# Output stage of a hybrid decoder step: weight loads issued by ScalarE's queue instead of SyncE's

## The chip, the cores and the metric

One core of a Trainium2 chip. The metric is the device time of the whole program in microseconds, here the median of several runs; the profile is of one execution. The engines are named as the profile names them: PE (TensorE), PEld (its weight loads), DVE (VectorE), ACT (ScalarE), POOL (GpSimd) and SP (SyncE), which computes nothing and issues DMAs. Each engine works through its own instructions in order; an instruction that starts a DMA is one of them, and waits like any other until what it depends on is done.

## What is computed

One inference step of a decoder layer, for a prompt of 1024 tokens (with 16 meta tokens ahead of it) and for eight sampled sequences of 4 tokens. Two branches, stick-breaking attention and gated linear attention, share one input projection and one output projection:

```
h = rms_norm(x, norm_pre_g)
(q, k, v), sg, (gq, gk, gv, gf), gg = branch_inputs(h, w_in, w_alpha, b_alpha)
o_sb = sb_prompt(q, k, v, sb_bias)            # sb_sample for the sampled rows
o_gla, s_end = gla_prompt(gq, gk, gv, gf)
mixed = concat([o_sb * silu(sg), rms_norm(o_gla) * silu(gg)])
x = x + rms_norm(mixed @ w_out, norm_post_g)  # 1024 x 2048 @ 2048 x 2048, fp32
```

The outputs are y for both, and the new keys, values and states. The change is in the stage that computes `mixed @ w_out` and the last norm.

## The kernel before

The program projects, runs both branches, and ends with the output stage (from L1282, some 360 us of 2080). The gated rows of the prompt lie in DRAM as `md`, in blocks of 128 x 512 that hold `mixed` transposed.

**Seven products in place of eight.** The output is cut in 2 x 2 blocks, and the block product is done by seven products p, in the order 1, 2, 6, 5, 3, 7, 4, each for two column halves q of 512. Their right sides are blocks of `w_out` (p = 1, 2, 3) or differences of such blocks that an earlier stage left in DRAM as `td` (p = 5, 6, 7, 4); their left sides are "forms" (`form`, L1357): blocks of `md`, or sums of them, loaded by SP in `quarter` (L1291, tiles q).

**fp32 in three passes.** Each fp32 operand is split in a high part, a CAST on ACT, and a low part, the rest, a subtraction on DVE: L1339 and L1342 for a form, L1400 and L1401 for a weight tile. `product` (L1594 to 1596) multiplies high by high, high by low, and low by high.

**A step (p, q)** is `step` (L1600): eight values of k, and for each the function `weights` and twelve products of 128 x 512 in four PSUM banks (t = 0 to 3). `weights` takes one of four `wr` buffers (`oy` pool, 128 x 512 fp32, 256 KB), loads the weight tile into it (L1395), casts it (L1400) and subtracts (L1401) into one of four slots of `ring`. In steps with p = 1, 2, 7 and 3, every second k is followed by eight small products for the sampled rows (L1614, tile `sc`) that read the two raw `wr` tiles; these buffers are free only behind them. In the other steps a `wr` buffer is free after its subtraction. Such a step of two k is a "sampled pair" below.

**Evacuation.** After eight k, `take` reads the four banks: for p = 1 copies on ACT (L1444), for p = 2 DVE and ACT (L1448), for p = 4 an addition on DVE (L1465) and `done` (L1435 on ACT, L1436 on DVE). The next product with the same banks waits for that.

**What runs beside it.** `finish0` (L1508 to 1538) normalizes the first half of the rows during p = 7 and p = 4: it loads x (L1519, L1522), does L1529 on DVE and stores (L1530). `load_keep` runs `weights` eight times more, for p = 4 and q = 1, into tiles of their own ("kept" loads), so that the last step finds its weights ready; the tail (from `take_last`) works row block by row block. `gain` (L1425) loads the norm's factors. All these DMAs are issued by SP; only one store at the very end (L1588) is ACT's.

**What sets the order.** A scheduler orders the instructions of each engine at build time by data dependence and priority; `weights` runs under `urgent()`, a higher priority. `behind_ring` sets kept loads and x loads behind the newest ring load where both are on one engine's list. Four first loads of the stage (`firsts`, L1318) were issued earlier.

Of the kernel before, what the change touches and what calls it, by code (L numbers as in the profile page):

```python
# [84 lines left out]
def hybrid_step(ctx: ExitStack, tc: tile.TileContext, x_prompt, x_sample, cache_k, cache_v, state_gla,  # L85
# [3 lines left out]
    nc = tc.nc  # L89
# [3 lines left out]
    def urgent():  # L93
        return tc.high_priority(offset=URGENT)
# [97 lines left out]
    with tc.tile_pool(name="xp", bufs=2) as xp, tc.tile_pool(name="xps", bufs=5, space=PSUM) as xps:  # L192
# [109 lines left out]
        for c, (lo, hi) in enumerate(XCHUNKS):  # L302
            n = hi - lo
            for k in range(NK):
                ps = xps.tile([P, 512], F32, tag="tx", name=f"tx{c}_{k}")
                ks = slice(k % 8 * P, (k % 8 + 1) * P)
                for j, i in enumerate(TILES[c]):
                    xt = xts[i]
                    if len(xt) == 2:
                        src, ii = xt[k // 8][:, ks], ident[:]  # L310
                    else:
                        rs = slice(64 * (k // 8), 64 * (k // 8) + 48)
                        src, ii = xt[0][rs, ks], ident[rs, rs]
                    nc.tensor.transpose(ps[:, j * P:min((j + 1) * P, n)], src, ii)
                ins = act.activation(hh[k][:, lo:hi], ps[:, :n], AF.Copy, scale=gpre[:, k:k + 1]).ins
# [967 lines left out]
    with ExitStack() as out:  # L1283
# [90 lines left out]
        def behind_ring(ins):  # L1374
            tc.add_manual_dep(ins, newest[0].name, NOSYNC, reason="behind")
# [3 lines left out]
        def weights(p, q, k, dst=None):  # L1379
            with urgent():  # L1380
                to_ring = dst is None
                if to_ring:
                    j = next(turn) % 4
                    dst = [t[:, j * 512:(j + 1) * 512] for t in ring]
                wh, wl = dst
                if firsts:
                    r = firsts.pop(0)
                else:
                    r = oy.tile([P, 512], F32, tag="wr", name=f"wr{p}{q}_{k}")[:]
                    if p <= 3:  # L1390
                        r0, c0 = (1024 if p > 1 else 0) + P * k, (1024 if p == 3 else 0) + 512 * q
                        src = w_out[0, r0:r0 + P, c0:c0 + 512]
                    else:
                        src = td[{5: 0, 6: 1, 7: 2, 4: 3}[p]][:, k, q * 512:(q + 1) * 512]
                    ins = nc.sync.dma_start(r, src).ins  # L1395
                    if to_ring:
                        newest[:] = [ins]
                    else:
                        behind_ring(ins)
                act.copy(wh, r)  # L1400
                vec.tensor_tensor(wl, r, wh.bitcast(F32), ALU.subtract)  # L1401
            return wh, wl, r
# [197 lines left out]
        def step(p, q, banks, first, last):  # L1600

            c = {1: 0, 2: 0, 7: 1, 3: 1}.get(p)
            if p in (1, 3):
                SB[c, q] = ops.tile([P, 512], F32, tag="S", bufs=2, name=f"sc{c}{q}")
            raws = []
            for k in range(8):
                w = weights(p, q, k)
                for t in range(4):
                    product(banks[t], t, p, k, w[:2], first, last)
                if c is not None:  # L1610
                    raws.append(w[2])
                    if k % 2:
                        for j in range(4):
                            mm(SB[c, q][32 * j:32 * j + 32, :256], small[SAMPLE[p]][:, k - 1 + j // 2, :],  # L1614
                               raws[j // 2][:, j % 2 * 256:j % 2 * 256 + 256], start=p in (1, 3) and k == 1,
                               stop=p in (2, 7) and k == 7, skip_group_check=True)
                        raws = []
                W.beat()
            for t in range(4):
                take(p, q, t, banks[t])  # L1620
            if p in (2, 7):
                sample_y(SB[c, q], 2 * c + q)
# [3 lines left out]
        def load_keep():  # L1626

            keep.extend(slot(REGION["B"][i], f"keep{i}") for i in range(4))
            for k in range(8):
                kept.append(weights(4, 1, k, [keep[k // 2][:, (2 * (k % 2) + i) * 512:(2 * (k % 2) + i + 1) * 512] for i in range(2)])[:2])  # L1630
                yield 3
# [55 lines left out]
```

## Time and profile before

| | us |
|---|---|
| median of 3 runs | 2083.68 (2082.94 to 2086.64) |
| profiled execution, device time | 2083.24 |
| its span in the trace | 2081.5 |
| granted PE clock, mean | 0.998 |
| output stage, steps in full use of PE | 1722 to 1963 |
| steps p = 7 and p = 4 (q = 0), p = 7 (q = 1) | 1963 to 2046 |
| last step and tail | 2046 to 2081.5 |

Times of rows are microseconds from the start of the span. A timeline row reads: start, duration, engine, line, operation, output and input tiles, shapes, how many instructions the row stands for, and in brackets how long the engine was idle before it and what ended that. SPq and ACTq are the queues' own rows: the time that the engine spends to issue a DMA, not the transfer. A row of waits reads: engine and line that waited, for which engine, tile and line, microseconds in all, times, the longest.

### The profile page before, as it was taken

The numbers are of one execution on the slowest core, as the hardware profiler recorded it, in microseconds if no ns is written. First come the engines' busy times: TensorE is split into PE (matmuls) and PEld (weight loads), VectorE is DVE, ScalarE is ACT, GpSimd is POOL, SyncE is SP. The second block draws the span as 40 slices with busy tenths as digits, with TensorE's granted clock in tenths as the row PEclk, the third lists the DMA queues.
The fourth block names the chain that finished last, engine by engine and source line by source line (L and its number), as shares of the span: only waits on it lengthen the run. The fifth ranks groups of instructions, "written<-read, shape, count | busy, mean of one in ns | idle before, by whom it ended". The sixth has DMA issues, their size and how long they took to land.

```text
span 2081.5 us, 42052 instructions
## 1 busy us (share of the span) xinstructions
PE 2047.1 (98%) x12547; PEld 1861.3 (89%) x12547; DVE 1553.6 (75%) x6284; ACT 958.5 (46%) x2286; POOL 83.9 (4%) x303
## 2 busy tenths in 40 slices
PE   6999999999999999999999999999999999999997
PEld 5999999999999989999999999998888898787775
DVE  7368989889888989899898888978444346553566
ACT  7355555565655656433535345253433335442332
POOL 0012000101000010000000000000000000000000
PEclk9999999999999999999999999999999999999999
DMA  6355454555554442533333434335777765442376
GB/s 200 105 135 151 134 159 135 159 136 151 146 159 144 143 115 79 143 96 85 108 98 84 121 76 119 82 92 162 236 226 239 222 214 188 138 151 83 127 247 212
DMA packets 372878, 301.86 MB, mean 145 GB/s; under 512 B 44440, under 2 KB 313160, under 8 KB 372648
## 3 DMA queue, kind: packets, MB, share of 16 engines
q1 hardware_dynamic: 372344, 298.64, 49.2%
q8 instruction: 99, 1.62, 0.3%
q14 instruction: 131, 1.07, 0.2%
q10 hardware_dynamic: 304, 0.53, 0.1%
HBM read 241.75 MB, written 57.31 MB: 144 GB/s over the span
## 4 chain that ended last, share of the span: by engine, by line
PE 89%; DVE 6%; DMA 3%; ACT 2%; issue 1%; POOL 0%; SPq 0%; DVEq 0%; ACTq 0%; POOLq 0%
PE acc_g L344 6%; PE acc_g L345 6%; PE acc_g L346 6%; PE b L1594 4%; PE b L1595 4%; PE b L1596 4%; PE acc_k L344 3%; PE acc_k L345 3%; PE acc_k L346 3%; PE acc_q L344 3%; PE acc_q L345 3%; PE acc_q L346 3%; PE acc_v L344 3%; PE acc_v L346 2%; PE acc_v L345 2%; PE acc_gv L344 2%
## 5 line engine op out<-in xcount | busy, mean ns | idle before, releaser
L463 DVE SCALAR_TENSOR_TENSOR jk<-kp,qb 128x128 f32<-128x128 f32 x2048 | 591.9, 289 | 41.8 <-DMA qb<-qsd 1.1
L344 PE MATMUL acc_g<-hT,wh_g 128*128 128x368 f32 (+2 forms) x768 | 251.2, 327 | 0.0
L345 PE MATMUL acc_g<-hT,wh_g 128*128 128x368 f32 (+2 forms) x768 | 247.3, 322 | 0.0
L346 PE MATMUL acc_g<-hT,wl_g 128*128 128x368 f32 (+2 forms) x768 | 247.0, 322 | 0.0
L1594 PE MATMUL b<-ring,f 128*128 128x512 f32 x416 | 166.2, 401 | 3.5 <-DVE u L1465 1.8
L463 DVE DVE_READ_ACCUMULATOR jk<-kp,qb 128x1 f32 x2048 | 166.5, 81 | 0.0
L1595 PE MATMUL b<-ring,f 128*128 128x512 f32 x416 | 163.3, 392 | 0.7 <-DVE ring L1401 0.6
L1401 DVE TENSOR_TENSOR ring<-wr,ring 128x512 fp32r<-128x512 f32 x104 | 70.7, 689 | 124.7 <-ACT ring L1400 124.4
L1596 PE MATMUL b<-ring,f 128*128 128x512 f32 x416 | 162.9, 392 | 0.0
L344 PEld LDWEIGHTS acc_g<-hT,wh_g 128*128 128x128 f32 x768 | 144.3, 188 | 12.7 <-issue 11.0
L345 PEld LDWEIGHTS acc_g<-hT,wh_g 128*128 128x128 f32 x768 | 144.4, 188 | 1.1 <-issue 0.4
L346 PEld LDWEIGHTS acc_g<-hT,wl_g 128*128 128x128 f32 x768 | 144.3, 188 | 0.0
L1400 ACT CAST ring<-wr 128x512 fp32r<-128x512 f32 x104 | 64.0, 621 | 159.5 <-DMA wr<-in_w_out_dram 74.2
L344 PE MATMUL acc_gv<-hT,wh_gv 128*128 128x384 f32 (+1 forms) x384 | 129.9, 338 | 0.0
L344 PE MATMUL acc_k<-hT,wh_k 128*128 128x378 f32 (+1 forms) x384 | 127.6, 332 | 0.0
L344 PE MATMUL acc_q<-hT,wh_q 128*128 128x368 f32 (+2 forms) x384 | 125.4, 326 | 0.0
L345 PE MATMUL acc_k<-hT,wh_k 128*128 128x378 f32 (+1 forms) x384 | 125.4, 326 | 0.0
L346 PE MATMUL acc_k<-hT,wl_k 128*128 128x378 f32 (+1 forms) x384 | 125.2, 326 | 0.0
L346 PE MATMUL acc_gv<-hT,wl_gv 128*128 128x384 f32 (+1 forms) x384 | 124.5, 324 | 0.0
L345 PE MATMUL acc_gv<-hT,wh_gv 128*128 128x384 f32 (+1 forms) x384 | 124.5, 324 | 0.0
L345 PE MATMUL acc_q<-hT,wh_q 128*128 128x368 f32 (+2 forms) x384 | 123.6, 322 | 0.0
L346 PE MATMUL acc_q<-hT,wl_q 128*128 128x368 f32 (+2 forms) x384 | 123.5, 322 | 0.0
(447 smaller groups left out, 5295.8 us busy)
## 6 DMA issues: line engine op xcount, KB each, us to landing
kp<-in_cache_k_dram SPq DMA_DIRECT2D x512, 64.0 KB
vr<-in_cache_v_dram SPq DMA_DIRECT2D x64, 512.0 KB
tf<-in_w_out_dram SPq DMA_DIRECT2D x64, 256.0 KB
td<-tf SPq DMA_DIRECT2D x64, 256.0 KB
qb<-qsd SPq DMA_DIRECT2D x64, 256.0 KB
wr_g<-in_w_in_dram SPq DMA_DIRECT2D x64, 256.0 KB
wr<-td SPq DMA_DIRECT2D x64, 256.0 KB
wr<-in_w_out_dram SPq DMA_DIRECT2D x48, 256.0 KB
```

Source lines behind the costliest of these rows:

```text
L344: mm(acc[c][:, :n], wh, hh[k][:, lo:hi], start=(k == 0), stop=False)
L345: mm(acc[c][:, :n], wh, hl[k][:, lo:hi], start=False, stop=False)
L346: W.mark = mm(acc[c][:, :n], wl, hh[k][:, lo:hi], start=False, stop=(k == NK - 1)).ins
L463: ins = vec.scalar_tensor_tensor(jk[:], kp[:], 1.0, qbs[h, b][:, t, :], ALU.mult, ALU.mult, accum_out=zt[:, t, NPG - 1 - i:NPG - i])
L1400: act.copy(wh, r)
L1401: vec.tensor_tensor(wl, r, wh.bitcast(F32), ALU.subtract)
L1594: mm(bk[:], ah, wh, start=first and k == 0, stop=False, skip_group_check=True)
L1595: mm(bk[:], ah, wl, start=False, stop=False, skip_group_check=True)
L1596: mm(bk[:], al, wh, start=False, stop=last and k == 7, skip_group_check=True)
```

## The change

One line in `weights`: the load of a weight tile is issued by ACT instead of SP.

```
@@ -1392,7 +1392,7 @@
                         src = w_out[0, r0:r0 + P, c0:c0 + 512]
                     else:
                         src = td[{5: 0, 6: 1, 7: 2, 4: 3}[p]][:, k, q * 512:(q + 1) * 512]
-                    ins = nc.sync.dma_start(r, src).ins
+                    ins = nc.scalar.dma_start(r, src).ins
                     if to_ring:
                         newest[:] = [ins]
                     else:
```

108 loads of 256 KB move, 100 for the ring and 8 kept ones; the four of `firsts` stay on SP. The loads of forms, of x and of factors, and the stores, stay on SP too. SP's list goes from 3460 rows to 3352 and ACT's from 2157 to 2265.

On ACT, at the end of step p = 1 and the start of p = 2 (both q = 0). `f_3` is the last form tile of p = 2, `wr_7` the last weight tile of p = 1, `wr_0` and `wr_1` the first of p = 2; + is the kernel after.

```order
+L1339 CAST f_2_29395<-q_5_29422 128x512
 L1400 CAST ring_29253<-wr_7_29447 128x512
-L1339 CAST f_2_29395<-q_5_29422 128x512
 L1339 CAST f_3_29442<-q_6_29443 128x512
 L1339 CAST f_3_29442<-q_7_29467 128x512
+L1395 DMA wr_0_29481<-in_w_out_dram 128x512
+L1395 DMA wr_1_29497<-in_w_out_dram 128x512
 L1400 CAST ring_29253<-wr_0_29481 128x512
 L1400 CAST ring_29253<-wr_1_29497 128x512
```

The two loads now stand behind three casts of form 2; the four copies of L1444 follow the two casts of `wr_0` and `wr_1`, as before.

On SP, near the end of step p = 7, q = 1. `wr_7` with `td_128` is the last kept tile, `wr_6` and `wr_7` with `td_127` are the last ring tiles; `xr` and `xrs` are rows of x, and the stores to `out_dram` are finished rows.

```order
 L1519 DMA xr_2_31548<-in_x_prompt_dram 128x512
 L1530 DMA out_dram<-y_1_2_30997 128x512
-L1395 DMA wr_7_31541<-td_128 128x512
-L1395 DMA wr_6_31550<-td_127 128x512
+L1530 DMA out_dram<-y_0_3_30659 128x512
 L1522 DMA xrs_31422<-in_x_prompt_dram 128x512
 L1519 DMA xr_3_31569<-in_x_prompt_dram 128x512
-L1530 DMA out_dram<-y_0_3_30659 128x512
-L1395 DMA wr_7_31571<-td_127 128x512
 L1522 DMA xrs_31421<-in_x_prompt_dram 128x512
```

The loads are no longer behind a store on SP, and the next store moves up two places.

On ACT at the same place.

```order
 L1400 CAST ring_29253<-wr_4_31500 128x512
 L1400 CAST ring_29253<-wr_5_31521 128x512
+L1395 DMA wr_7_31541<-td_128 128x512
+L1395 DMA wr_6_31550<-td_127 128x512
 L1400 CAST keep_31048<-wr_7_31541 128x512
 L1400 CAST ring_29253<-wr_6_31550 128x512
+L1395 DMA wr_7_31571<-td_127 128x512
 L1400 CAST ring_29253<-wr_7_31571 128x512
 L1435 ACTIVATE jk_3_31595,yssq<-y_1_0_30796 128x512
```

The last kept load and the last two ring loads are issued between the casts, the very last one behind the cast of the tile before it.

More of the change, by code (lines that the diff above doesn't have):

```diff
@@ L1394, in weights @@
                         src = td[{5: 0, 6: 1, 7: 2, 4: 3}[p]][:, k, q * 512:(q + 1) * 512]
-                    ins = nc.sync.dma_start(r, src).ins
+                    ins = nc.scalar.dma_start(r, src).ins
                     if to_ring:
```

## The prediction

> **What bounds the kernel now.** I read the busy table of the page first, then the output stage cut into pieces by a table of windows, and then the waits of the queue that issues the loads. TensorE (PE) is busy nearly all the time.
>
> ```profile
> PE 2047.1 (98%) x12547; PEld 1861.3 (89%) x12547; DVE 1553.6 (75%) x6284; ACT 958.5 (46%) x2286; POOL 83.9 (4%) x303
> ```
>
> The change touches only the output stage, from about 1722 us on. Each row of the windows gives a stretch, then its length, then for PE, its weight loads, DVE, ACT and POOL the busy time, then the granted PE clock, the DMA share and GB/s.
>
> ```profile
> 1722.00:1963.00 241.00, 241.00 (x1187) 187.73 (x1185) 125.48 (x205) 93.64 (x177) 0.20 (x1) 1.00 0.42 134
> 1963.00:2046.00 83.00, 78.77 (x373) 57.86 (x366) 49.09 (x82) 28.13 (x60) 0.00 (x0) 0.98 0.73 237
> 2046.00:2072.10 26.10, 25.79 (x118) 20.15 (x117) 22.65 (x59) 7.13 (x24) 0.00 (x0) 1.00 0.54 184
> 2040.00:2045.00 5.00, 3.87 (x11) 2.86 (x12) 2.37 (x4) 1.35 (x3) 0.00 (x0) 0.75 0.71 218
> 2045.00:2050.00 5.00, 5.00 (x26) 3.54 (x25) 3.64 (x7) 2.10 (x6) 0.00 (x0) 0.91 0.98 311
> ```
>
> The reader is to see three things. In the first 241 us PE has no idle time (241.00 of 241.00), so an earlier load can win nothing there and a later one can only lose. The p=7 and p=4 steps, 1963 to 2046, hold 83.00 - 78.77 = 4.2 us of idle PE, and at the end of them a stretch of lowered clock (0.75, then 0.91), where PE counts as busy but is slow. After 2046 nothing that the change moves is left.
>
> SP issues all loads before. Rows: who waited, for what, us in all, times, longest.
>
> ```profile
> SPq L1395 <- PE sc L1614: 93.1, 27, 10.1
> SPq L1395 <- DVE ring L1401: 69.7, 42, 5.1
> SPq L1530 <- DVE y L1529: 8.1, 3, 4.0
> ```
>
> SP's waits at L1395 are mostly waits for a free buffer, which is no fault of SP: whichever queue issues the load has to wait for the same matmuls. Only the third row is time in which a store holds up loads that might have gone.
>
> **The change, part by part.** The issue itself: SP spends 319 to 333 ns on most of its loads, and ACT's own DMA at the end took 0.38 us.
>
> ```profile
> L1395 SPq DMA_DIRECT2D wr<-td x64: 319/320/1316, 1826.3 to 2040.9; - x64
> L1395 SPq DMA_DIRECT2D wr<-in_w_out_dram x44: 327/333/1937, 1738.7 to 1957.5; - x44
> 2077.35 0.38 ACTq L1588 DMA_DIRECT2D out_dram<-y  x1
> ```
>
> 108 loads (64 + 44; four more stay on SP) at 0.32 to 0.38 us are 35 to 41 us that go from SP to ACT. ACT is busy for 93.64 of 241 us and 28.13 of 83 us, so it has 202 us free beside PE's work and the time itself fits. What is not free is the order: ACT now stands at a load until its buffer is free, and casts and bank copies behind it wait, while a load stands behind casts that wait for other data. The slowest issues (1316 and 1937 ns) could come on either queue; I count them alike.
>
> *Term 1, end of step p=1 q=0 and start of p=2.* The order of the changed kernel puts loads 0 and 1 of p=2 on ACT behind the last two CASTs of form 2, and the four copies that empty the banks stay behind the casts of these loads. Before (SP, ACT, and the sampled products of PE):
>
> ```profile
> 1745.39 0.85 SPq L1395 DMA_DIRECT2D wr<-in_w_out_dram  x2
> 1751.22 0.80 SPq L1395 DMA_DIRECT2D wr<-in_w_out_dram  x2
> 1757.70 0.81 SPq L1395 DMA_DIRECT2D wr<-in_w_out_dram  x2
> 1751.35 1.98 ACT L1339 CAST f<-q 128x512 fp32r<-128x512 f32 x3
> 1755.59 0.62 ACT L1400 CAST ring<-wr 128x512 fp32r<-128x512 f32 x1 [2.26 <-DMA wr<-in_w_out_dram]
> 1756.89 2.04 ACT L1444 COPY u<-b 128x512 f32<-128x512 f32 x4
> 1757.04 0.64 PE L1614 MATMUL sc<-wr,small 128*32 128x256 f32 x8
> 1757.61 0.50 PE L1594 MATMUL b<-ring,f 128*128 128x512 f32 x1
> ```
>
> SP issued at 1751.22; ACT would be free of its three CASTs at 1751.35 + 1.98 = 1753.33, so the load starts 2.1 us later. The first cast came 1755.59 - 1751.22 = 4.37 us after its issue, so it comes at 1757.7, and the first copy 1.3 us behind it (1756.89 - 1755.59) at 1759.0 instead of 1756.89. PE's product at 1757.61 overwrites that bank, and the copy had ended only 0.2 us ahead of it. So this place loses 2.1 - 0.2 = 1.9 us. If the form's casts come 1.3 us sooner, as their data may once SP's queue holds no loads, 0.6 is left; if the next pair of loads, which then stands behind the 2.04 us of copies instead of 1757.70, uses up its reserve as well, it is some 3.5. **I take +1.9, bounds 0.6 to 3.5.**
>
> *Term 2, the other sampled pairs* (every two k of p=1, 2, 3 and 7; 21 of them outside terms 1 and 3). One from step p=1 q=1, before:
>
> ```profile
> 1813.86 1.91 SPq L1395 DMA_DIRECT2D wr<-in_w_out_dram  x2
> 1813.30 1.14 ACT L1339 CAST f<-q 128x512 fp32r<-128x512 f32 x2 [1.11 <-PE b L1596]
> 1817.18 0.62 ACT L1400 CAST ring<-wr 128x512 fp32r<-128x512 f32 x1 [2.74 <-DMA wr<-in_w_out_dram]
> 1817.83 0.69 DVE L1401 TENSOR_TENSOR ring<-wr,ring 128x512 fp32r<-128x512 f32 x1 [2.09 <-ACT ring L1400]
> 1820.34 0.39 PE L1595 MATMUL b<-ring,f 128*128 128x512 f32 x1
> ```
>
> The low half is ready at 1817.83 + 0.69 = 1818.52 and PE needs it at 1820.34, a reserve of 1.8 us. A load that must pass the two CASTs at 1813.30 would go at 1814.44, 0.6 later than SP's. If it had to pass both in full it would be 1.14 + 0.38 = 1.5 us, still inside 1.8. The cover is this reserve; beyond it each 0.1 us in 21 pairs is 2.1 us. The steps without samples have more room, since their buffers come free earlier. **I take +0.2, bounds 0 to 6.3** (0.3 us over in every pair).
>
> *Term 3, steps p=7 and p=4.* Here SP sends stores of finished rows and loads of x between the weight loads, in order. At the last place:
>
> ```profile
> 2032.63 0.64 PE L1614 MATMUL sc<-wr,small 128*32 128x256 f32 x8
> 2034.25 0.34 SPq L1530 DMA_DIRECT2D out_dram<-y  x1
> 2034.70 0.86 SPq L1395 DMA_DIRECT2D wr<-td  x2
> 2039.50 0.62 ACT L1400 CAST keep<-wr 128x512 fp32r<-128x512 f32 x1 [6.68 <-DMA wr<-td]
> 2040.23 0.62 ACT L1400 CAST ring<-wr 128x512 fp32r<-128x512 f32 x1
> 2040.15 0.69 DVE L1401 TENSOR_TENSOR keep<-wr,keep 128x512 fp32r<-128x512 f32 x1 [4.02 <-ACT keep L1400]
> 2040.90 0.49 PE L1594 MATMUL b<-ring,f 128*128 128x512 f32 x1 [1.39 <-ACT ring L1400]
> 2041.62 0.50 PE L1595 MATMUL b<-ring,f 128*128 128x512 f32 x1 [0.23 <-DVE ring L1401]
> 2042.43 0.58 PE L1595 MATMUL b<-ring,f 128*128 128x512 f32 x1
> 2045.80 0.43 PE L1594 MATMUL b<-ring,f 128*128 128x512 f32 x1
> ```
>
> The buffers were free when the sampled products ended, at 2032.63 + 0.64 = 2033.27; the loads went at 2034.70 because the store ahead of them waited for DVE. On ACT nothing is ahead of them (its CASTs had ended), so they go 1.4 us earlier, and the cast that PE waits for comes at 2038.8. The stall was 1.39 us, and the step to the low half took 0.72 us instead of the 0.34 of other places, 0.4 more; of these 1.8 about 0.2 is left. The eight products from 2042.43 to 2045.80 took 3.37 us where 8 x 0.227 = 1.8 is usual, so the lowered clock cost 1.55, which goes with the stall. That is -3.1. Then the next load is late: it takes the buffer that DVE gives back after the keep subtraction (2040.15 + 0.69, now 1.4 earlier, 2039.4), needs 3.1 us to land and 0.62 for its cast, and PE asks for it 2.72 us after 2039.5: 2043.1 against 2042.2, +0.9. So this place gives -2.2.
>
> [...]
>
> The other stalls of the stage, by their rows:
>
> ```profile
> 2016.59 0.62 ACT L1400 CAST keep<-wr 128x512 fp32r<-128x512 f32 x1 [5.41 <-DMA wr<-td]
> 2021.18 0.50 PE L1594 MATMUL b<-ring,f 128*128 128x512 f32 x1 [1.17 <-DVE u L1465]
> 2022.76 0.50 PE L1594 MATMUL b<-ring,f 128*128 128x512 f32 x1 [0.62 <-DVE u L1465]
> 1985.48 0.50 PE L1594 MATMUL b<-ring,f 128*128 128x512 f32 x1 [0.36 <-ACT ring L1400]
> ```
>
> The two of 1.17 and 0.62 follow from the kept load at 2016.59, behind which the cast of another ring load stood; that cast now goes ahead of it, but the bank's DVE additions (L1465) still stand behind the stores' arithmetic, so I take a third of their 1.8 off, -0.6. The one at 1985.48 goes, and a load of the same step that must pass a cast in its place costs as much: 0. In p=4 q=0 two L1435 passes now stand ahead of load 2: +0.3. **Term 3: -2.2 - 0.6 + 0.3 = -2.5, bounds -5.8 (all 4.2 of idle time and 1.55 of low clock) to +1** (the new order's stalls without the gain at the end).
>
> Sum: +1.9 + 0.2 - 2.5 = **-0.4 us**. On the profiled execution, 2083.24 us with its span of 2081.5, that is 2082.8; its own time lies 0.44 below the median of the three runs (2083.68), and on that median it is 2083.3, which I forecast.
>
> **The rivals.** (1) *All of the last stage's stalls go.* For it: the stage is the one place with idle PE, and DMA there is dense (0.73 of the engines), so loads that go their own way may also land sooner than behind SP's stores. Against: the buffers' releases and DVE's order are unchanged. Time: -5.8 + 0.6 = -5.2, 2078.5. [...]
>
> (2) *Slower, the ring runs behind.* Place: the 21 sampled pairs. Mechanism: ACT reaches a load late because a cast in front of it waits for its q tile or for a slot, and the load after it, its cast and the next load all follow on the same engine. It decides from a delay of 1.8 us per pair on. At 0.3 over it, 21 x 0.3 = 6.3, with +1.9 and a smaller gain of -1 in the end: +7.2, 2090.9. For it: the order does put a CAST ahead of the load in most of these steps. Against: 1.5 us is what two such casts cost.
>
> (3) *Slower, the first place at its bound and no gain at the end:* 3.5 + 1 = +4.5, 2088.2. It decides if the first cast of p=2 comes after 1759 and a stall of over 1 us stays before 2046.
>
> (4) *The loads are not sooner, whoever issues them:* SP's waits (93.1 and 69.7 us) are for buffers, and what is left is term 1: +1.9, 2085.6. [...]
>
> **How the numbers follow.** Chances: forecast 0.40, rival 1 0.19, rival 2 0.15, rival 3 0.16, rival 4 0.10. Within 0.2% (4.2 us, about what a measurement of this kernel tells from no change) lie the forecast and rival 4: 0.50; faster 0.19, slower 0.31. The range from 2078.3 to 2089.5 takes in rivals 1, 3 and 4 and the milder half of rival 2; left out are its rest and larger gains, under 2 in 10. The forecast's own range is 2080 to 2087.
>
> **What would show it.** In the profile of the changed kernel: the first L1444 copy starts about 2 us later against the sampled products before it, and PE idles 1 to 3 us there (term 1). In the rest of the stretch up to the p=5 and p=3 steps PE stays without idle time; idle time of a few tenths at each sampled pair means rival 2. In the p=7 and p=4 stretch the two loads near its end go right after the sampled products, the granted clock stays at 1.00, and a stall near 0.9 us comes one k later (term 3); if the clock still falls, the gain is nearly lost. A change of over 1 us after p=4's last ring product, or ACT issues much longer than 0.4 us, would make the whole working wrong.

## The result, and the profile after

| | before | after |
|---|---|---|
| median, us (lowest to highest, runs) | 2084.72 (2082.94 to 2089.36, 6) | 2095.14 (2090.84 to 2095.7, 6) |
| profiled execution, device time, us | 2083.24 | 2094.73 |
| its span, us | 2081.5 | 2092.8 |
| granted PE clock, mean | 0.998 | 0.998 |

The ratio of after to before is 1.0047, interval 1.0037 to 1.0057: slower by 0.47%, 9.8 us. That lies outside the predicted range, on the side that had a chance of 0.31.

The busy table of after shows PE with 2.3 us more work than before and the span 11.3 us longer; so 9 us are new idle time, not all of it the change's (below).

```profile
PE 2049.4 (98%) x12547; PEld 1861.3 (89%) x12547; DVE 1554.0 (74%) x6284; ACT 959.4 (46%) x2286; POOL 83.8 (4%) x303
```

The windows of after (columns as in the prediction). Its steps come up to 11 us later than before, so the cuts are set around the same stalls and not at the same times:

```profile
1722.00:1763.00 41.00, 36.42 (x194) 28.31 (x192) 28.37 (x51) 21.03 (x40) 0.15 (x1) 1.00 0.64 202
1763.00:1963.00 200.00, 199.48 (x960) 154.61 (x960) 98.01 (x157) 72.61 (x136) 0.00 (x0) 1.00 0.39 123
1963.00:2055.00 92.00, 83.95 (x400) 61.05 (x396) 49.86 (x83) 29.38 (x62) 0.00 (x0) 1.00 0.65 212
2055.00:2060.00 5.00, 4.64 (x12) 3.31 (x12) 2.54 (x4) 1.53 (x5) 0.00 (x0) 0.66 0.95 290
```

PE was never idle from 1722 to 1963 before. Now 4.6 us are idle in the first 41 us, then 0.5 in 200 us. Of the 4.6, two waits of 0.8 and 1.1 us (1727.87 and 1736.01) end before the first load that moves is issued; e3, which moves nothing there, has the second one too (1.1 us). The p = 7 and p = 4 steps have 92.00 - 83.95 = 8.0 us of idle time instead of 4.2, and the stretch of low clock still comes, only later (0.66 at 2055). The middle is as forecast; both ends are not.

What PE waits for from 1722 us on, from the table of waits (us, times, longest), first in before, then in after, here with ACT's own waits for the transfers of `td`:

```profile
PE b L1594 <- DVE u L1465: 1.8, 2, 1.2
PE b L1594 <- ACT ring L1400: 1.7, 2, 1.4
PE b L1595 <- DVE ring L1401: 0.6, 3, 0.2
```

```profile
PE b L1594 <- ACT ring L1400: 4.5, 3, 2.5
PE b L1594 <- ACT u L1444: 2.5, 1, 2.5
PE b L1595 <- DVE ring L1401: 2.2, 4, 0.9
PE b L1594 <- DVE u L1465: 2.1, 2, 1.9
PE b L1594 <- ACT gx L520: 1.1, 1, 1.1
ACT ring L1400 <- DMA wr<-td: 42.2, 24, 5.0
```

Two rows make most of the growth: casts of ring tiles, 4.5 us instead of 1.7, and the bank copies of step p = 1 (L1444), 2.5 instead of none. The subtractions behind the casts (L1595's row) add 1.6. The row of L520 is the wait of 1.1 us ahead of the change.

**Where each microsecond came in.** For every kernel below, the start of PE's first L1594 product of each k was set against the same product of before, and the growth of that distance taken over four pieces of the program. The first piece ends at k = 4 of p = 1, ahead of the first load that moves; the second goes on to k = 2 of p = 2; the third to the first step with p = 7; the fourth to the end of the span.

| kernel | ratio to before | ahead of the change | first place | middle | last stage | all |
|---|---|---|---|---|---|---|
| after | 1.0047 | 2.24 | 3.85 | 0.02 | 5.19 | 11.3 |
| e1_first | 1.0022 | 2.26 | 5.13 | 0.00 | 0.71 | 8.1 |
| e2_mid | 1.0001 | 1.07 | -0.09 | 0.74 | 0.27 | 2.0 |
| e3_last | 1.0019 | 3.89 | 0.50 | 0.00 | 4.49 | 8.9 |
| e5_form_later | 1.0029 | 1.82 | 1.19 | 0.49 | 1.43 | 4.9 |
| e6_ring74 | 1.0043 | 0.35 | 0.04 | 0.00 | 8.22 | 8.6 |
| e7_keep | 1.0018 | -0.02 | 0.36 | 0.00 | 3.35 | 3.7 |
| e8_store_pool | 1.0015 | 1.62 | -0.06 | 0.00 | 3.42 | 5.0 |
| e9_keep2_ahead | 1.0024 | 0.50 | 1.53 | 0.78 | 5.90 | 8.7 |
| e10_late | 0.9995 | -0.12 | -0.24 | 0.00 | -0.16 | -0.5 |
| e11_last_nostore | 0.9989 | 0.47 | 0.38 | 0.00 | -3.54 | -2.7 |
| e12_before_nostore | 0.9975 | 3.31 | 0.27 | 0.00 | -3.36 | 0.2 |

The column ahead of the change goes from -0.1 to 3.9 us over kernels that do the same up to there. It is chance of single executions, and so 2.2 of after's 11.3 us are not the change's; 11.3 - 2.2 = 9.1 agrees with the 9.8 of the ratio. The other columns vary by chance, too: in the kernels that move nothing at the first place it goes from -0.2 to 0.5, and in e1 and e2, which move nothing in the last stage, that is 0.7 and 0.3. The ratios are from several runs of each kernel, the other columns from one execution.

**The first place in after** (ACT, its issues, PE). Bracketed is the idle time before a row and what ended it.

```profile
1755.64 1.29 ACT L1339 CAST f<-q 128x512 fp32r<-128x512 f32 x2
1756.37 0.82 ACTq L1395 DMA_DIRECT2D wr<-in_w_out_dram  x2
...
1761.25 0.62 ACT L1400 CAST ring<-wr 128x512 fp32r<-128x512 f32 x1 [4.32 <-DMA wr<-in_w_out_dram]
1762.88 0.58 ACT L1444 COPY u<-b 128x512 f32<-128x512 f32 x1
...
1754.14 0.50 PE L1594 MATMUL b<-ring,f 128*128 128x512 f32 x1 [0.36 <-ACT ring L1400]
1754.95 0.50 PE L1595 MATMUL b<-ring,f 128*128 128x512 f32 x1 [0.30 <-DVE ring L1401]
1760.39 0.64 PE L1614 MATMUL sc<-wr,small 128*32 128x256 f32 x8
1763.52 0.50 PE L1594 MATMUL b<-ring,f 128*128 128x512 f32 x1 [2.49 <-ACT u L1444]
```

The sampled products serve as the clock here. Before, the loads went 1757.04 - 1751.22 = 5.82 us ahead of them, now 1760.39 - 1756.37 = 4.02: 1.8 later. The first cast comes 4.88 us after the issue instead of 4.37, and the first copy 1.63 after that cast instead of 1.30. Together the copy is 2.6 us later against PE, and PE waits 2.49 us for it.

**The last stage in after**, k = 7 of the first p = 7 step (ACT and its issues, PE, SP's issues):

```profile
1992.13 0.33 ACTq L1395 DMA_DIRECT2D wr<-td  x1
1997.57 0.62 ACT L1400 CAST keep<-wr 128x512 fp32r<-128x512 f32 x1 [4.02 <-DMA wr<-td]
2001.63 0.62 ACT L1400 CAST ring<-wr 128x512 fp32r<-128x512 f32 x1 [3.43 <-DMA wr<-td]
2002.30 0.73 PE L1594 MATMUL b<-ring,f 128*128 128x512 f32 x2 [2.47 <-ACT ring L1400]
...
1991.45 0.46 SPq L1519 DMA_DIRECT2D xr<-in_x_prompt_dram  x1
1992.00 5.34 SPq L1530 DMA_DIRECT2D out_dram<-c  x2
```

The kept load issued at 1992.13 is cast 5.4 us later. Ring load 7 goes into the buffer that this cast and its subtraction free; it is cast at 2001.63, and PE stands for 2.47 us. Beside the kept load SP issues a load of x at 1991.45 and a store at 1992.00.

The end of the last p = 7 step in after:

```profile
2043.62 0.64 PE L1614 MATMUL sc<-wr,small 128*32 128x256 f32 x8
2044.35 0.81 ACTq L1395 DMA_DIRECT2D wr<-td  x2
2048.81 0.62 ACT L1400 CAST ring<-wr 128x512 fp32r<-128x512 f32 x1 [0.27 <-DMA wr<-td]
2049.29 0.33 ACTq L1395 DMA_DIRECT2D wr<-td  x1
2054.47 0.62 ACT L1400 CAST ring<-wr 128x512 fp32r<-128x512 f32 x1 [5.04 <-DMA wr<-td]
2055.14 0.50 PE L1594 MATMUL b<-ring,f 128*128 128x512 f32 x1 [1.69 <-ACT ring L1400]
2055.86 0.79 PE L1595 MATMUL b<-ring,f 128*128 128x512 f32 x1 [0.22 <-DVE ring L1401]
```

The pair of loads goes 0.1 us after the sampled products, as forecast, and PE no longer waits at k = 6 (-1.46 us against before). But the one load behind it, issued at 2049.29, is not ready for its cast until 2054.47. PE waits 1.69 + 0.22 us for it, one k later than before, and the low clock follows that wait (0.66 in the window above).

### The profile page after: what moved, and what is told of

Its sections match the earlier page's. It is cut to its first block, busy times and chain, and to the rows that moved or that the text cites. A ratio compares the mean times of both kernels' runs of the same rounds, so it can differ in the third digit from the quotient of the medians.

```text
span 2092.8 us, 41981 instructions
## 1 busy us (share of the span) xinstructions
PE 2049.4 (98%) x12547; PEld 1861.3 (89%) x12547; DVE 1554.0 (74%) x6284; ACT 959.4 (46%) x2286; POOL 83.8 (4%) x303
## 3 DMA queue, kind: packets, MB, share of 16 engines
q8 instruction: 99, 1.62, 0.3%
q14 instruction: 131, 1.07, 0.2%
## 4 chain that ended last, share of the span: by engine, by line
PE 82%; DVE 8%; DMA 5%; ACT 2%; issue 2%; POOL 0%; SPq 0%; DVEq 0%; ACTq 0%; POOLq 0%
PE acc_g L344 5%; PE acc_g L345 5%; PE acc_g L346 5%; PE b L1594 4%; PE b L1595 4%; PE b L1596 4%; PE acc_k L344 3%; PE acc_q L344 3%; PE acc_k L345 3%; PE acc_k L346 3%; PE acc_q L345 3%; PE acc_q L346 3%; PE acc_v L344 3%; DVE jk L463 3%; PE acc_v L346 2%; PE acc_v L345 2%
## 5 line engine op out<-in xcount | busy, mean ns | idle before, releaser
L1594 PE MATMUL b<-ring,f 128*128 128x512 f32 x416 | 166.3, 401 | 10.3 <-ACT ring L1400 4.5
L1595 PE MATMUL b<-ring,f 128*128 128x512 f32 x416 | 163.7, 394 | 2.4 <-DVE ring L1401 2.2
```

Of the source, the lines that this page charges most:

```text
L1594: mm(bk[:], ah, wh, start=first and k == 0, stop=False, skip_group_check=True)
L1595: mm(bk[:], ah, wl, start=False, stop=False, skip_group_check=True)
```

## The experiments

Two theories, which some expectations call A and B. **The order (A):** a load on ACT stands behind casts that wait for other data, and casts stand behind a load that waits for its buffer. **Sharing (B):** with the weight loads gone from SP's list, SP's stores and x loads no longer wait for their turn behind them; transfers of both queues are under way together, and a weight load lands later. The first group cuts the change in three parts of the program; the form of the edit is always that of the first one.

**e1_first: only the 12 loads of p = 1 and p = 2, q = 0.**

```
-                    ins = nc.sync.dma_start(r, src).ins
+                    ins = (nc.scalar if p < 3 and q == 0 else nc.sync).dma_start(r, src).ins
```

> Only the 12 ring loads of p=1 and p=2, q=0, that are not issued early go through ACT; the other 96 stay on SP. Theory A (a load on ACT stands behind casts that wait for other data): the loss of the changed kernel at this place, which its trace has as 3.85 us (from 2.24 to 6.09 late between k=4 of p=1 and k=2 of p=2), comes back whole, +3 to +5 us on the time, and PE's first product of p=2 again waits over 2 us for a copy of L1444; the last stage stays as before. Theory C (what differs is chance of the runs, or lies ahead of the first moved load, where the changed kernel's trace is already 2.2 us late): within 1 us of before.

Measured: 2089.82 (2087.99 to 2092.41, 11 runs) beside 2085.06 (29 runs); ratio 1.0022, interval 1.0013 to 1.0030. PE's rows show the same wait at the same place:

```profile
1763.19 0.51 PE L1594 MATMUL b<-ring,f 128*128 128x512 f32 x1 [2.36 <-ACT u L1444]
```

The first place alone costs some 0.22%, 4.6 us. (In this profile it is 5.13 us against 3.85 in after, because here the granted clock fell behind the wait: 0.66 from 1763 to 1768, with products 0.43 us apart from 1764.33 to 1766.89 where 0.23 us is usual.)

**e2_mid: only the 64 loads between** (condition `p in (6, 5, 3) or p < 3 and q == 1`).

> Only the loads from p=1, q=1 to p=3, q=1, except the 4 of p=7 (64 loads) go through ACT. Theory A: in the trace of the changed kernel these steps keep step with before to 0.02 us, so 0, within 1 us; PE without idle time from 1766 to 1963. The rival of the forecast (each sampled pair a little late because ACT reaches its loads late): +2 to +6 us. Theory B (loads land later wherever SP's queue is no longer held up): 0 here too, there is little beside them.

Measured: 2085.47 (2083.17 to 2088.27, 11 runs); ratio 1.0001, interval 0.9993 to 1.0010. A window over this part:

```profile
1775.00:1963.00 188.00, 187.54 (x899) 145.66 (x899) 93.23 (x150) 68.33 (x130) 0.00 (x0) 1.00 0.39 122
```

Idle time is 0.5 us in 188. The reserves hold; 64 of the 108 loads move for nothing, in either sense.

**e3_last: only the 32 loads of p = 7 and p = 4** (condition `p in (7, 4)`).

> Only the loads of p=7 and p=4 (32, the 8 kept ones among them) go through ACT. Theory A: the changed kernel's loss in this stage, 3.7 us up to the last ring tile and 1.6 behind it by the later stretch at half clock, comes back: +4 to +6 us, with a stall of over 2 us at k=7 of the first p=7 step. Theory C: within 1.5 us of before. With the run of only the first loads on ACT the two should add up to the loss of the changed kernel, less what lies ahead of the first moved load.

Measured: 2089.46 (2085.69 to 2092.7, 12 runs); ratio 1.0019, interval 1.0010 to 1.0028. The last stage alone costs 4 us where a gain was forecast. The three parts add up to 0.22 + 0.01 + 0.19 = 0.42%, close to 0.47%. PE's wait at k = 7 of the first p = 7 step is there too:

```profile
2000.34 0.73 PE L1594 MATMUL b<-ring,f 128*128 128x512 f32 x2 [3.12 <-ACT ring L1400]
```

**e4_pool: all 108 loads issued by POOL** (`nc.gpsimd.dma_start`), an engine that has nothing else to do here; by the order theory the loss should go with ACT's casts out of the way.

> All 108 loads through POOL's queue, which has nothing else to do in this stage: off SP as in the changed kernel, but behind no cast. Theory A: the stall at the start of p=2 shrinks to under 1 us and the one at k=7 of the first p=7 step to under 1.5 us; time between -4 and +2 us of before, unless an issue on POOL is itself slow (then every sampled pair shows it). Theory B (the loads land late because SP's stores and x loads, no longer held behind them, share the DMA engines with them): as slow as the changed kernel in the last stage, +4 us or more there.

Measured: 2213.08 (2211.61 to 2216.55, 5 runs); ratio 1.0617, interval 1.0602 to 1.0632. It tells nothing of the theories, since POOL brings a cost of its own. Its rows:

```profile
1834.99 0.55 POOL L1395 DMA_DIRECT2D wr<-in_w_out_dram  x1 [4.44 <-PE sc L1614]
1838.76 0.54 POOL L1395 DMA_DIRECT2D wr<-in_w_out_dram  x1 [3.21 <-issue]
1842.35 0.54 POOL L1395 DMA_DIRECT2D wr<-in_w_out_dram  x1 [3.04 <-issue]
```

The two loads that wait for nothing the profile shows start 3.8 and 3.6 us after the one before; over all 61 such loads it is 3.2 us at least and 3.55 in the median, too slow for a ring that uses a tile every 2.7 us (twelve products, 0.227 us apart in before).

**e5_form_later: the change, and the last two casts of form 2 behind loads 2 and 3 of p = 2.** It takes two of the three casts out of the way of loads 0 and 1.

```
-                t = slot(REGION[HOME[p]][i], f"f{p}_{i}")
+                t = slot(REGION[HOME[p]][i], f"f{p}_{i}") if p != 2 or i < 3 else (yield 4) or slot(REGION[HOME[p]][i], f"f{p}_{i}")
...
-                    split(f[:, 0], f[:, 1], combined(p, k), evacs[-1] if p == 2 else None)
+                    split(f[:, 0], f[:, 1], combined(p, k), (evacs[-1] if i < 3 else newest[0]) if p == 2 else None)
```

> The changed kernel, with one thing moved: the two CASTs of the last tile of form 2 stand behind loads 2 and 3 of p=2, q=0 on ACT, so loads 0 and 1 no longer stand behind them. Theory A (order on ACT): the wait of PE's first product of p=2 for the L1444 copy falls from 2.5 us to under 0.8, and the time from about +9.8 us over before to +7 or +8. Theory B (the loads land late, 4.9 us after their issue, because SP's form loads run beside them): the wait stays over 2 us and the time at +9 to +10.

Measured: 2089.73 (2088.24 to 2099.37, 11 runs) beside 2085.89 (28 runs); ratio 1.0029, interval 1.0017 to 1.0041. The place, in ACT's and PE's rows:

```profile
1759.99 0.58 ACT L1444 COPY u<-b 128x512 f32<-128x512 f32 x1
1760.62 0.50 PE L1594 MATMUL b<-ring,f 128*128 128x512 f32 x1 [0.69 <-ACT u L1444]
1761.90 1.17 ACT L1339 CAST f<-q 128x512 fp32r<-128x512 f32 x2
```

With the casts behind the copies, the wait falls from 2.49 to 0.69 us and the first place from 3.85 to 1.19. So the order on ACT is what costs there. The ratio gives 0.18% back, more than was expected (0.29% is 6.0 us, not 7 or 8), but its interval overlaps after's.

**e6_ring74 and e7_keep: e3's loads in two halves,** the 24 ring loads (condition `p in (7, 4) and to_ring`) and the 8 kept ones (condition `not to_ring`).

> Of the loads of p=7 and p=4 only the 24 ring loads go through ACT; the 8 kept ones stay on SP. Theory A, in the form that a kept load stuck behind a ring cast on ACT delays the next ring load that takes its buffer: the loss of 4.0 us (all 32 on ACT) falls to between 0 and 2, and the stall at k=7 of the first p=7 step to under 1.5 us. Theory B (SP's stores and x loads crowd the ring loads once these leave SP's queue): still +3 to +5.

> Only the 8 kept loads go through ACT, all others stay on SP. Theory A in the same form: kept load 2 again waits behind the cast of ring load 5 on ACT, and ring load 7, which waits for its buffer, is late: a stall of 2 us or more at k=7 of the first p=7 step and +2 to +4 us in all. If the ring loads' own place on ACT is what costs: within 1 us of before.

Measured: e6 2094.37 (5 runs), ratio 1.0043, interval 1.0030 to 1.0056; e7 2089.61 (11 runs), ratio 1.0018, interval 1.0007 to 1.0028. e6, 0.43% or 9.0 us, missed both ranges, though the wait at k = 7 of the first p = 7 step fell to 1.2 us: ring loads alone cost more than ring and kept loads together. e7's 0.18%, 3.7 us, lies in the range of theory A, but not by its place: PE waits only 0.1 us at k = 7 of the first p = 7 step. Its loss came at the start of the last p = 7 step, where the products of k = 1 and 2 come 3.8 us later, behind DVE:

```profile
2025.79 0.79 PE L1594 MATMUL b<-ring,f 128*128 128x512 f32 x1 [3.04 <-DVE u L1465]
```

e6 loses 3.8 us at the same place, also behind L1465, though DVE's delay there comes from a kept tile's cast in e6 and from a load of x in e7. A kept load behind a cast on ACT is thus not enough to explain the wait at k = 7.

**e8_store_pool: before, with the 16 stores of `finish0` on POOL.** Nothing of the weights is moved; they only lose the stores ahead of them.

```
-                nc.sync.dma_start(y_prompt[0, i * P:(i + 1) * P, b * 512:(b + 1) * 512], o)
+                nc.gpsimd.dma_start(y_prompt[0, i * P:(i + 1) * P, b * 512:(b + 1) * 512], o)
```

> Before, with only the 16 stores of finished rows (L1530) issued by POOL, so that SP's weight loads never stand behind a store's wait; the weight loads stay on SP. If the prediction's term 3 had the right cause for the stall near the end (a store that waits for DVE ahead of the loads on SP): the stall at k=6 of the last p=7 step, 1.4 us with the half clock behind it, goes and the time is 1 to 4 us under before. If the next load is late in its place: within 1 us.

Measured: 2089.17 (2087.55 to 2089.97, 11 runs); ratio 1.0015, interval 1.0006 to 1.0024. The gain at the end is there (-2.7 us at k = 6 and 7 of the last p = 7 step), but 6.2 us are lost at its k = 1 and 2, so neither expectation was met. DVE's row, then PE's:

```profile
2023.72 0.75 DVE L1529 SCALAR_TENSOR_TENSOR y<-y,r_y,xr 128x512 f32<-128x512 f32 x1 [2.84 <-DMA xr<-in_x_prompt_dram]
2027.00 0.80 PE L1594 MATMUL b<-ring,f 128*128 128x512 f32 x1 [4.63 <-DVE u L1465]
```

DVE now stands at a step of `finish0` that waits for x, with the bank's addition behind it, as in e7: a transfer late, and an engine's order that passes it on to PE. The last ring load went 3.0 us sooner than before, counted from the sampled products of k = 5, and took 4.44 us to land instead of 3.08, on SP's queue.

**e9_keep2_ahead: e5, with kept load 2 set ahead of the cast of ring tile 5 on ACT.** This is the order theory's own cure for the wait at k = 7.

```
-                        behind_ring(ins)
+                        behind_ring(ins); k != 2 or tc.add_manual_dep(casts[7, 0, 5], ins.name, NOSYNC, reason="behind")
...
-                act.copy(wh, r)
+                cast = casts[p, q, k] = act.copy(wh, r).ins
```

> The kernel of e5 (all loads on ACT, form 2's last casts later) with kept load 2 put ahead of ring cast 5 of the first p=7 step on ACT; in the three traces with all loads of this stage on ACT it was issued within 0.02 us of that cast's start, which waits for a landing. Theory A: kept load 2 goes 1.5 to 2 us sooner, and the loss at k=7 of the first p=7 step and k=0 of p=4, 5.4 us in e5 beside before, falls to 1 to 3 (1.5 to 1.7 stood there with all loads of the stage on SP, too); the time falls by 2 to 3 us under e5's, to +3 over before. Theory B (landing times of 5 to 6 us behind SP's stores decide): the loss stays at 4 or more.

Measured: 2091.05 (2085.91 to 2092.52, 11 runs) beside 2084.91 (21 runs); ratio 1.0024, interval 1.0014 to 1.0035. Rows of ACT and PE:

```profile
1984.12 2.33 ACTq L1395 DMA_DIRECT2D wr<-td  x3
1987.02 0.62 ACT L1400 CAST ring<-wr 128x512 fp32r<-128x512 f32 x1 [3.01 <-DMA wr<-td]
1992.51 0.62 ACT L1400 CAST keep<-wr 128x512 fp32r<-128x512 f32 x1 [0.86 <-DMA wr<-td]
...
1998.51 1.22 PE L1594 MATMUL b<-ring,f 128*128 128x512 f32 x2 [3.31 <-ACT ring L1400]
```

The kept load went at 1985.98, 1.04 us ahead of the cast that it stood behind, and PE's wait at k = 7 is still 3.31 us. The order on ACT alone does not explain this place. The landings (issue, queue, what, last part landed, and the time between), worked out from the trace's issue and completion events, of e9 and of e2, where all of this is on SP:

```
e9  1985.61 ACT ring load 6   1991.00  5.39     e2  1983.78 SP ring load 6   1988.86  5.08
    1985.98 ACT kept load 2   1992.48  6.51         1984.14 SP kept load 2   1989.51  5.36
    1986.04 SP  store         1991.16  5.12         1984.67 SP x load        1990.13  5.46
    1986.43 SP  x load        1992.64  6.21         1985.20 SP store         1990.80  5.60
    1986.94 SP  store         1993.12  6.18
```

In e2, with one queue, these transfers land in the order of issue, 0.62 to 0.67 us apart. In e9, with two, the kept load is overtaken by a store that was issued 0.06 us after it, and lands 6.51 us after its issue.

The kept load and the x load of the other queue land 0.16 us apart, though they were issued 0.45 apart.

**e10_late: only the last three loads,** those of the one place where the prediction saw its gain (condition `q and (p == 7 and k > 5 or p == 4 and k == 7)`).

> Before, with only three loads on ACT: the last kept one and the last two ring loads (k=6 and 7) of the last p=7 step; PE's and DVE's orders are those of before. This is the place that the prediction's term 3 worked out: the two loads go 1.4 us sooner, the stall of 1.39 us at k=6 goes, with the half clock behind it, and k=7 is about 0.9 late: -2.2 us, between -3.5 and -0.5 on the time. If the half clock comes behind the next stall instead: within 1 us.

Measured: 2083.85 (2082.36 to 2088.83, 11 runs) beside 2084.91 (21 runs); ratio 0.9995, interval 0.9985 to 1.0004. Rows of ACT and PE, then a window:

```profile
2033.07 0.84 ACTq L1395 DMA_DIRECT2D wr<-td  x2
2038.24 0.34 ACTq L1395 DMA_DIRECT2D wr<-td  x1
2042.79 0.62 ACT L1400 CAST ring<-wr 128x512 fp32r<-128x512 f32 x1 [4.62 <-DMA wr<-td]
2043.46 0.49 PE L1594 MATMUL b<-ring,f 128*128 128x512 f32 x1 [1.29 <-ACT ring L1400]
2044.18 0.50 PE L1595 MATMUL b<-ring,f 128*128 128x512 f32 x1 [0.23 <-DVE ring L1401]
```

```profile
2045.00:2050.00 5.00, 5.00 (x22) 3.43 (x21) 3.73 (x6) 2.59 (x7) 0.00 (x0) 0.70 0.95 305
```

The wait at k = 6 goes (-1.46 us), and comes back at k = 7: the last load lands 4.53 us after its issue (2038.24 to 2042.76), where it took 3.08 before (2040.87 to 2043.95). The low clock moves behind it (0.70). The product of k = 7 still starts 2.05 us sooner than before, close to the -2.2 of the prediction; from there to the end 1.80 are lost again, behind the low clock. Nothing is gained that the runs can tell from no change.

**e11_last_nostore and e12_before_nostore: e3 and before, both without 15 of the 16 stores of `finish0`,** so that these rows of the output are not written.

```
-                nc.sync.dma_start(y_prompt[0, i * P:(i + 1) * P, b * 512:(b + 1) * 512], o)
+                if n == 15: nc.sync.dma_start(y_prompt[0, i * P:(i + 1) * P, b * 512:(b + 1) * 512], o)
```

> The kernel of e3 (all 32 loads of p=7 and p=4 on ACT) without 15 of the 16 stores of finished rows (those outputs are not written), so that 15 of SP's transfers of 256 KB no longer run beside the weight loads; ACT's order is that of e3. To be read beside e12. Theory B (the weight loads share the DMA engines with SP's stores and x loads, which no longer stand behind them): the excess of the ACT version over its own SP version, 4.0 us with stores, falls to under 1.5. Theory A (ACT's order, whatever the transfers): it stays at 3 to 5.

> Before without the same 15 stores (those outputs are not written); all weight loads on SP. The base for e11. The stalls behind SP's waits for stores go: 1 to 5 us under before. The first p=7 step at k=7 and the last at k=6 then show what is left without stores.

Measured beside 2086.09 (19 runs): e11 2082.32 (11 runs), ratio 0.9989, interval 0.9980 to 0.9998; e12 2081.43 (9 runs), ratio 0.9975, interval 0.9965 to 0.9985. PE's wait at k = 7 of the first p = 7 step of e11, and the window of the last stage in e11 and in e12:

```profile
1993.83 0.73 PE L1594 MATMUL b<-ring,f 128*128 128x512 f32 x2 [0.45 <-ACT ring L1400]
```

```profile
1963.00:2046.00 83.00, 80.68 (x387) 59.06 (x385) 50.90 (x86) 29.44 (x63) 0.00 (x0) 1.00 0.60 190
```

```profile
1963.00:2046.00 83.00, 80.19 (x387) 60.62 (x386) 50.32 (x84) 29.36 (x62) 0.00 (x0) 0.98 0.59 188
```

With the stores gone, the wait of 3.12 us in e3 is 0.45, and PE's idle time in the stage is 2.3 us with the loads on ACT and 2.8 with them on SP. In the profiles, moving the loads cost 4.49 us in this stage with the stores there, and -3.54 + 3.36 = -0.2 without them. The times of many runs do not bear that out: 0.14% between e11 and e12 (2.9 us; 0.9 by the medians) against e3's 0.19%, each with an interval of about 0.1% either way. By the ratios the loss without stores lies between the two expectations, by the medians in that of theory B, so neither is confirmed.

Nor does the shorter wait show that sharing was its cause. Worked out from the issue and completion events as above, in us from the end of the sampled products of k = 3 of the first p = 7 step:

| | kept load 2 issued | landed | ring load 7 issued | landed | PE's wait at k = 7 |
|---|---|---|---|---|---|
| e2 (SP) | 0.39 | 5.75 | 7.16 | 10.06 | 1.11 |
| e3 (ACT) | 1.64 | 7.81 | 9.21 | 12.50 | 3.12 |
| e9 (ACT, kept load ahead) | 0.40 | 6.91 | 8.47 | 12.24 | 3.31 |
| e12 (SP, no stores) | 0.44 | 3.42 | 4.83 | 7.52 | 0 |
| e11 (ACT, no stores) | 2.07 | 5.42 | 6.82 | 9.53 | 0.45 |

ACT makes ring load 7 land 2.4 us later with the stores (e3 beside e2) and still 2.0 later without them (e11 beside e12). The wait shrinks because everything lands some 2.5 to 3 us sooner without the stores, on either queue, and PE has room for the delay. In e11 most of the delay is order (the kept load goes 1.6 later), in e9 all of it is landing (1.15 for the kept load, 0.87 for ring load 7), in e3 it is both. So the place and its chain are shown. Later landings alone are enough for the wait (e9), and the order delays ring load 7 almost as much where the stores are gone (e11); how the loss divides between them with both present is not settled.

No run beat before with the full output by more than its interval.

## Why the prediction was wrong, point by point

**Term 1 (predicted +1.9, bound 3.5; measured 3.85 in the profile, 0.22% or 4.6 us by e1).** The mechanism is the one forecast, the size is not. The delay of the issue was right (1.8 us, 2.1 worked out). Mis-sized were the landing and the copy behind it, taken as before: they came 0.5 and 0.3 us later, which makes a wait of 2.49 us. And three smaller lags at k = 5 to 7 of p = 1, 1.1 us together, were not in the sum at all. Two of them are the waits of 0.36 and 0.30 in the rows. Those loads also moved to ACT, but kernels that leave them on SP have up to 0.5 us there as well. e5 took most of the term away by moving two casts.

**Term 2 (predicted +0.2; measured 0.02, and e2 1.0001).** Right. The reserve of 1.8 us per sampled pair covers the order on ACT, and rival 2 did not happen.

**Term 3 (predicted -2.5; measured +5.2 in the profile, 0.19% or 4 us by e3).** This is the step that failed, in two ways.

*The last place, "so this place gives -2.2".* The store's 1.4 us did go, and the wait at k = 6 with it. (It also went where these loads stayed on SP but PE came there later, e1 and e12, so only e10 shows it for the move alone.) What failed is "the lowered clock cost 1.55, which goes with the stall". The stall was to come back one k later as 0.9 us; it came back as 1.29 + 0.23 in e10 and 1.69 + 0.22 in after, and the clock fell behind it, so the 1.55 us booked as won did not come. The landing in that sum, "needs 3.1 us to land", was wrong as well: 4.53 us in e10 and 5.15 in after (2049.29 to 2054.45). In e10 that was nearly made up by luck, since the load also went 1.2 us sooner than worked out (2038.24 instead of 2039.4). The longer landing is not ACT's alone: on SP's queue the same load took 4.23 us in e1 and 4.44 in e8, and without stores 2.77 (e11, ACT) and 2.93 (e12, SP). The 3.1 was read from a load with two transfers unfinished ahead of it; in e10 and in after there were five. Against before the place gave -1.46 at the start of k = 6, -0.19 to that of k = 7 and +1.95 from there to the end, +0.3 us in all.

*The rest of the stage, "-0.6 + 0.3".* The first p = 7 step was put at nothing ("costs as much: 0"), and it is the largest loss: 3.9 us in after.

- k = 7 of that step costs 2.6 us. With the k behind it the place costs 2.7 us in after, 5.4 in e3 and e5 and 6.2 in e9; 1.6 to 2.3 of the latter three come in the k behind, at a low clock that after was spared. In any other run it is 1.9 at most, and it varies by chance: 1.7 and 1.6 in e1 and e2, which move nothing there. The kept load's buffer is the one that ring load 7 waits for, so a kept tile that is late there, by order or by landing, is passed on whole.
- 0.64 us at k = 0 comes from PE's own order: with these loads on ACT, two of the eight sampled products stand ahead of k = 1, and after, e3, e5, e9 and e11 all lose the same 0.64 there. No expectation had it.
- 0.6 us come at k = 3 to 5, behind a wait of 0.94 us for a subtraction.

In p = 4 q = 0, load 2 did stand behind the two L1435 passes (it goes at 2006.19, right behind them) and cost 1.1 us in after instead of 0.3, but nothing in e3. The third of 1.8 us was not won: the two waits for L1465 are 1.91 and 0.23 in after.

The prediction costed what ACT does with the loads, and not what SP does without them. SP stood at weight loads for 163 us in all before; freed of that, it issues part of its stores and x loads sooner (the sixth to eighth store 3.3 to 9.6 us, counted from the start of the stage), beside the weight loads instead of behind them. The mean time from issue to landing of the stage's 32 weight loads hardly moved: 3.92 us before, 3.82 and 3.94 in e1 and e2, 4.06 in after and 4.15 in e3; without stores 3.37 (e12) and 3.56 (e11). The longest did: 5.4 to 5.9 us in before, e1 and e2, and 6.3 to 7.3 in after, e3, e5 and e9. The bounds "-5.8 to +1" of this term allowed a loss of 1 us at most, and that was too narrow.

**The rivals.** Rival 3 had the right places and the right sign, and half the size (4.5 us against 9.8): its first place was past the bound, and the last stage lost 4 to 5 us instead of 1. Rival 1's reason, that loads that go their own way may land sooner, did not hold: by the mean they landed no sooner, and the longest landings grew. In e9 a transfer of each queue landed close together (1991.00 and 1991.16, 1992.48 and 1992.64). The kept load landed behind SP's store, which was issued after it, and took 6.51 us instead of 5.36.

**What stays open.** Why ring loads alone on ACT (e6) cost more than ring and kept loads together (e3), and how the last stage's loss divides between order, later landings and SP's list running ahead of DVE, as in e7 and e8. The experiments settle the first place and the last; k = 7 of the first p = 7 step has two causes that no run parts, and the smaller losses between were not tested.

## What to carry to other kernels

A queue that several kinds of transfers share is also an order of precedence. Moving the urgent ones to another engine's queue puts them behind that engine's work (1.8 us at the first place of after), which the order of instructions shows ahead of time, and takes away what held the others back (the sixth to eighth store of the stage went 3.3 to 9.6 us sooner), which it does not show: ask of the old queue, too, what it will now send and when. And where a stall is to go, price the next load with a landing in the new company (5.15 us in after, where 3.1 was taken), since a stall that only moves one step on can bring its low clock along (0.66 in after).

## What the runs showed of the hardware

- Issued from POOL, 256 KB loads that waited for nothing shown started 3.55 us apart in the median, though the instruction itself took 0.54 us (e4).
- The length of a wait alone does not tell in these runs whether the granted clock falls. It fell after two waits with a product between of 1.39 + 0.23 us (before, 0.75), 1.69 + 0.22 (after, 0.66) and 1.29 + 0.23 (e10, 0.70), and after single waits of 3.12 us (e3, 0.66) and 2.36 (e1, 0.66), but not after those of 2.49 and 2.47 us in after (1.00 from 1763 to 1768 and from 2002 to 2007). What else decides it is not shown.
- The stretch at low clock was granted 0.50 from 2042.47 to 2045.88 us in before and from 2055.77 to 2059.19 in after, with 1.00 ahead of it and behind it.
- The same stretch of program ahead of the change took up to 4 us more in one execution than in another (3.89 in e3, -0.12 in e10, each against before).
